# The attention of two layers issued in an order written by hand, with pieces of the output projection between its steps

## The chip, the cores and the metric

The kernel runs on one core of a Trainium2 chip. Its engines work side by side: TensorE (PE) does matmuls and transposes, VectorE (DVE), ScalarE (ACT) and GpSimd (POOL) do arithmetic on tiles in SBUF and PSUM, and SyncE (SP) issues the transfers between DRAM and SBUF. Each engine takes its own instructions strictly in order, and an instruction waits until the semaphores it names have reached their values. The metric is the time of one execution in microseconds (us). Three runs of the kernel before gave 2439.22, 2440.98 and 2441.18 us; the median, 2440.98, is the time before.

## The reference

A trunk of two layers works on 1024 positions of 1024 channels in f32. A layer has two halves: a token mixer and a ConvFFN. Cut to the mixer:

```python
mod = (c_act @ w_ada[l] + b_ada[l])[:, None, :]
sh1, sc1, g1, sh2, sc2, g2 = jnp.split(mod, 6, axis=-1)
h = x * (1.0 + sc1) + sh1
z = h @ w_in[l] + b_in[l]
z_a, z_q, z_k, z_v, z_c = jnp.split(z, splits, axis=-1)
y_a = conformer_conv(z_a, ...)            # 256 wide
y_b = diff_attention(z_q, z_k, z_v, ...)  # 512 wide: 4 heads of 128
y_c = chunked_spatial_gating(z_c, ...)    # 256 wide
y = jnp.concatenate([y_a, y_b, y_c], axis=-1) @ w_out[l] + b_out[l]
x = layer_norm(DEEPNORM_ALPHA * x + (1.0 + g1) * y, ...)
```

The differential attention takes, for each of its four heads and each block of 128 queries, two causal softmax maps p0 and p1 over the keys up to that block, forms a = p0 - lambda * p1, multiplies by v, and normalises each row of the head's output by its root mean square. The ConvFFN then uses sh2, sc2 and g2 in the same way. The six parts of `mod` are called modulation 0 to 5.

## The kernel before

Matmuls run on 512 columns, and each f32 product is made of three (`mm3`: high by high, low by high, high by low), for which operands are split into a high and a low part: ScalarE casts the high part (L125), and POOL or VectorE subtracts it to get the low part (L126). So every weight tile of the output projection, `wout`, is loaded by a transfer on SP's queue (L681), multiplied on POOL by the gate row (L682), cast on ScalarE to `woh`, and subtracted on POOL to `wol`.

`stage1` makes the projections, the convolution and the gating, then q and k of heads 0 to 2, rotated and written to DRAM (`qk_head`: z, `rot`, VectorE at L520 to L524). Its background work (`self.bg`, advanced by `pump`) is a mix of the convolution's taps (L410) and, in layer 0, of modulations 2 and 4: for each modulation eight tiles `wada` of 512 KB are loaded and accumulated on VectorE into `macc` (the first at L258, the others at L260), and `modp` on PE sums the result.

`attention` is a generator that writes out one unit at a time. A unit is one head and one block of 128 queries, i from 0 to 7, with i + 1 key tiles. Its steps: scores `sc` on PE (L733, and a mask at L735), maxima `mx` on VectorE (L754 or L756), exponentials `p` with row sums on ScalarE (L759), the difference on VectorE (L762 to L767), transposes `at` on PE (L774) with copies on ScalarE (L775), the product with v, `pv`, on PE (L778), and two activations on ScalarE (L780, L781). The blocks come in the order 7, 6, 3, 5, 2, 4, 1, 0; in head 3 7, 6, 5, 4, 0, 1, 2, 3. After a head `head_end` normalises, and turns its output by PE transposes `obt` (L801). The heads' q and k come back from DRAM as `stq` and `stk`, v as `vp`. Modulation 3 of layer 0 is loaded and accumulated beside heads 1 to 3. In the midst of heads 2 and 3 the turned heads 0 and 1 (`ybr`, L811) and the four last `wout` are loaded and split.

`stage3` then writes out the rest: the first four `wout` tiles are split, residual rows `r` are loaded and in layer 0 added to a row `ab` on POOL (L871), and `out_fill` adds part of the output projection to them in 512-column halves: 16 pieces of 12 matmuls (`of`; operands `yah`, `yal`, `ych`, `ycl`), then 16 pieces of 6 (`ybh`, `ybL`), each followed by one VectorE operation (L862). What remains, `og`, belongs to the next stage (`boundary`). Head 3's k projection, `prf`, 48 matmuls, stands behind head 0's first unit.

This text order is not the order of issue. The framework's scheduler orders the instructions of all engines by priorities and by estimated times; the `fill` argument and `issue_after` guide it. So a matmul of a piece is put wherever the scheduler sees PE free.

## Time and profile before

| | |
|---|---|
| median of 3 runs | 2440.98 us |
| profiled execution | 2437.79 us |
| its span, first to last instruction | 2436.1 us |
| mean granted clock of PE | 0.974 |
| PE, DVE, ACT, POOL busy | 95%, 80%, 43%, 13% |
| attention of layer 0, first score to first `og` | 286.05 to 507.06 us |
| attention of layer 1, first score to first `og` | 1492.04 to 1708.22 us |

A row of the timeline gives start, length, engine, line, operation, output and inputs, and in brackets the idle time before it with what ended that. Matmul records overlap their successors, so the distance of two starts tells how long one occupies PE, and the sum of the records tells more than that. A row of the table by windows gives the stretch, its length, then the busy time of PE, PEld, DVE, ACT and POOL with counts, PE's granted clock (1.00 is full), the share of the DMA engines in use and GB/s. With a filter on a tile or an engine it counts only those instructions.

### The profile page before, as it was taken

The page shows a single profiled execution, that of the slowest core. Times are in us where ns is not written, and L with a number is a line of the kernel's source. Part 1 is how long each engine was busy: PE and PEld are TensorE (multiplying, and loading weights), DVE is VectorE, ACT ScalarE, POOL GpSimd, SP SyncE. Part 2 cuts the span into 40 slices and gives each one's busy share as a digit, 9 for nine tenths or more (in the row PEclk, how much of TensorE's full clock was granted, in tenths as well). Part 3 has the DMA queues.
Part 4 walks back from the last instruction along what each step waited for, and adds up shares of the span by engine and source line. Part 5 has one row for each costly group of instructions (what it writes and reads, how often), then busy time and mean ns, then how long its engine had stood idle before and what let it go on. Part 6 is the DMA issues. An engine that isn't in the chain of part 4 may idle for free.

```text
span 2436.1 us, 28260 instructions
## 1 busy us (share of the span) xinstructions
PE 2308.1 (95%) x10846; PEld 1886.4 (77%) x10846; DVE 1956.1 (80%) x2650; ACT 1049.9 (43%) x1692; POOL 328.9 (13%) x165
## 2 busy tenths in 40 slices
PE   8998999979999999999959999999899999999996
PEld 7787778767888887788848877777688888878885
DVE  7898876778887888877978988657987777797857
ACT  4214754646554555311130257555654555561111
POOL 1143260410000000000020541214100000000003
PEclk9998999999999999999979999999999999999998
DMA  7433462122332333745523244320232222254301
GB/s 294 156 116 120 140 224 104 61 95 90 110 113 88 112 113 121 263 141 179 190 70 117 78 143 160 130 95 27 99 100 87 78 78 87 87 176 169 122 26 69
DMA packets 87672, 294.06 MB, mean 121 GB/s; under 512 B 9265, under 2 KB 18801, under 8 KB 86001
## 3 DMA queue, kind: packets, MB, share of 16 engines
q1 hardware_dynamic: 87536, 292.26, 35.4%
q8 instruction: 85, 1.39, 0.2%
q14 instruction: 51, 0.41, 0.1%
HBM read 228.23 MB, written 64.00 MB: 120 GB/s over the span
## 4 chain that ended last, share of the span: by engine, by line
PE 67%; DVE 17%; issue 6%; ACT 4%; DMA 3%; POOL 2%; SPq 0%; POOLq 0%; DVEq 0%; ACTq 0%
PE upb L1083 6%; PE upb L1084 6%; PE upb L1085 6%; PE og L130 5%; PE og L131 5%; PE og L132 5%; PE sc L733 3%; PE upd L1084 3%; PE upd L1085 3%; PE upd L1083 3%; DVE convacc L410 2%; PE pv L778 2%; PE of L130 2%; PE of L132 2%; PE of L131 2%
## 5 line engine op out<-in xcount | busy, mean ns | idle before, releaser
L1083 PE MATMUL upb<-comb,uw 128*128 128x512 f32 x704 | 274.9, 391 | 9.9 <-DVE upc L1107 5.0
L130 PE MATMUL og<-dn,dn 128*128 128x512 f32 x704 | 275.3, 391 | 2.6 <-ACT r L885 2.1
L131 PE MATMUL og<-dn,dn 128*128 128x512 f32 x704 | 274.5, 390 | 0.0
L132 PE MATMUL og<-dn,dn 128*128 128x512 f32 x704 | 274.3, 390 | 0.0
L1084 PE MATMUL upb<-comb,uw 128*128 128x512 f32 x704 | 274.0, 389 | 0.0
L1085 PE MATMUL upb<-comb,uw 128*128 128x512 f32 x704 | 273.9, 389 | 0.0
L1107 DVE TENSOR_TENSOR uw<-wu,uw 128x512 fp32r<-128x512 f32 x210 | 144.1, 686 | 125.3 <-ACT uw L1110 125.3
L1120 DVE SCALAR_TENSOR_TENSOR cv<-upc,pc,cv 128x1023 f32<-128x1023 f32 (+1 forms) x176 | 225.4, 1280 | 2.9
L138 POOL TENSOR_TENSOR lnrs<-lnrs,mhalf 128x1 f32<-128x1 f32 x32 | 24.8, 779 | 1421.4 <-DVE lnrs L137 1414.9
L887 DVE TENSOR_TENSOR r<-og,r 128x1024 f32<-128x1024 f32 x128 | 155.7, 1218 | 59.0 <-PE og L132 58.4
L410 DVE SCALAR_TENSOR_TENSOR convacc<-convy,pc,convacc 128x1023 f32<-128x1023 f32 (+14 forms) x120 | 176.2, 1469 | 2.3
L125 ACT CAST dn<-actr 128x1024 fp32r<-128x1024 f32 x44 | 46.1, 1049 | 298.1 <-issue 224.4
L1083 PEld LDWEIGHTS upb<-comb,uw 128*128 128x128 f32 x704 | 132.1, 188 | 41.0 <-DVE upc L1107 6.7
L1110 ACT CAST uw<-wu 128x512 fp32r<-128x512 f32 x210 | 121.7, 616 | 83.6 <-DVE wu L1107 77.1
L130 PEld LDWEIGHTS og<-dn,dn 128*128 128x128 f32 x704 | 132.2, 188 | 31.5 <-ACT r L885 3.4
L1085 PEld LDWEIGHTS upb<-comb,uw 128*128 128x128 f32 x704 | 132.2, 188 | 27.5
L132 PEld LDWEIGHTS og<-dn,dn 128*128 128x128 f32 x704 | 132.2, 188 | 27.4
L1084 PEld LDWEIGHTS upb<-comb,uw 128*128 128x128 f32 x704 | 132.2, 188 | 27.2
L131 PEld LDWEIGHTS og<-dn,dn 128*128 128x128 f32 x704 | 132.2, 188 | 26.8
L1083 PE MATMUL upd<-comb,uw 128*128 128x512 f32 x352 | 137.3, 390 | 0.0
L1085 PE MATMUL upd<-comb,uw 128*128 128x512 f32 x352 | 136.9, 389 | 0.0
L1084 PE MATMUL upd<-comb,uw 128*128 128x512 f32 x352 | 136.9, 389 | 0.0
(312 smaller groups left out, 5474.4 us busy)
## 6 DMA issues: line engine op xcount, KB each, us to landing
wada<-in_w_ada SPq DMA_DIRECT2D x96, 512.0 KB, 4.6
wu<-in_w_up_t SPq DMA_DIRECT2D x84, 512.0 KB, 3.6
d_act<-cv SPq DMA_DIRECT2D x44, 512.0 KB, 2.6
actr<-d_act SPq DMA_DIRECT2D x44, 512.0 KB, 4.6
wdn<-in_w_down SPq DMA_DIRECT2D x44, 512.0 KB, 4.2
win<-in_w_fm SPq DMA_DIRECT2D x24, 512.0 KB, 4.0
wtm<-in_w_tm SPq DMA_DIRECT2D x16, 512.0 KB, 3.7
wout<-in_w_out SPq DMA_DIRECT2D x16, 512.0 KB, 6.2
```

The costliest lines, as they stand in the source:

```text
L130: mm(ps, lh, rh, start=first, stop=False)
L131: mm(ps, lh, rl, start=False, stop=False)
L132: mm(ps, ll, rh, start=False, stop=last)
L410: nc.vector.scalar_tensor_tensor(out=acc[:, d:], in0=y[:, :S - d], scalar=w(30 - d), in1=acc[:, d:], op0=ALU.mult, op1=ALU.add)
L733: nc.tensor.matmul(ps[m][:, c0:c1], q[ms, isl], k[ms, c0:c1], start=n == 0, stop=n == 2 and c1 != w)
L887: nc.vector.tensor_tensor(out=r[t], in0=ps, in1=r[t], op=ALU.add)
L1083: mm(ps, w[:, 0, ks], hi[k], start=k == 0 and not more, stop=False, skip_group_check=True)
L1084: mm(ps, w[:, 0, ks], lo[k], start=False, stop=False, skip_group_check=True)
L1085: mm(ps, w[:, 1, ks], hi[k], start=False, stop=k == 3, skip_group_check=True)
L1107: v.tensor_tensor(out=o, in0=x, in1=y, op=op)
L1110: act.copy(self.up_w[n][:, 0], src)
L1120: v.scalar_tensor_tensor(out=u[:, d:], in0=c[:, :S - d], scalar=self.ffw[:, 2 - d, m:m + 1], in1=u[:, d:], op0=ALU.mult, op1=ALU.add)
```

## The change

The whole attention is written out inside a block, `manual_schedule`, that makes PE, ScalarE and VectorE take their instructions in the order of the program text. The old unit is taken apart into functions: `att_score`, `att_max`, `att_exp`, `att_diff`, `att_turn`, `att_out`. A loop over 32 units (g = 0 to 31) issues, for unit g and the one before it, prev: scores(g), difference(prev), maxima(g), transposes(prev), exponentials(g), a piece, pv(prev), and for some units a second piece. The pieces are, in units 0 to 5, chunks of head 3's k projection (`key_chunks`); in 6 and 7 nothing; in 8 to 19 the 16 pieces of 12 matmuls, two each in 8, 10, 12 and 14; in 20 to 23 nothing; in 24 to 31 the 16 pieces of 6, two each. The late weight tiles and the turned heads 0 and 1 are loaded and split in units 20 to 23. `stage3` is gone.

In layer 0 modulation 4 leaves the background of `stage1` and goes behind modulation 3 in the attention: eight loads of 512 KB and eight VectorE accumulations, one step a unit from unit 8 on. SP and POOL are still ordered by the scheduler.

```diff
@@ -634,7 +634,7 @@
         self.drain_bg()
         if l == 0:
             self.mod_cfg = ("Rb", "Rb")
-            self.bg.append(self.mix(self.mods(0, (2, 4)), self.conv_taps(l, self.y[0], self.acc[0], 0)))
+            self.bg.append(self.mix(self.mods(0, (2,)), self.conv_taps(l, self.y[0], self.acc[0], 0)))
         else:
             self.bg.append(self.conv_taps(l, self.y[0], self.acc[0], 0))
         self.stage_v(l, H, O)
@@ -661,13 +661,14 @@
         self.lhs_a(O)
         vp = self.load_vp(l, 0)
         self.lhsB, self.lhs0, self.wB = [], [], []
-        self.at = O + "c"
-        att = self.attention(l, self.X, O, stk, vp, grow)
         self.qk_head(l, 3, H, O, 0, (0,))
-        next(att)
-        self.qk_head(l, 3, H, O, 0, (1,), True)
-        self.at = self.X + "c"
-        return att, grow
+        wk = self.load_win(l, ZT["k"] + 3, O + "b")
+        self.wA = []
+        with self.tc.manual_schedule(engines={nc.tensor.engine, nc.scalar.engine, nc.vector.engine}):
+            r = self.attention(l, H, self.X, O, stk, vp, grow, wk)
+        self.psum(3, 2)
+        self.up_first(l, O + "c")
+        return r, self.lhsB, self.wB[2:]
 
...
+    def att_max(self, u):
...
+    def att_score(self, u, stk):
+        u["w"] = (u["i"] + 1) * P
+        u["small"] = u["i"] < 4
+        if u["small"]:
+            ps2 = u["ps2"] = self.mm("sc")
+            u["ps"] = [ps2[:, 0:512], ps2[:, 512:1024]]
+        else:
+            u["ps"] = [self.mm("sc"), self.mm("sc")]
+        self.score(u["ps"], stk, u["i"])
+
+    def att_exp(self, u):
...
+    def att_diff(self, l, u):
...
+    def att_turn(self, u, at):
...
+    def att_out(self, u):
...
+    def head_norm(self, ot, ss, halves):
...
+    def head_scale(self, ot, ss, halves):
...
+    def head_turn(self, l, h, O, ot, halves):
...
+    def key_chunks(self, l, h, H, w):
+        nc = self.nc
+        m = ZT["k"] + h
+        hi, lo = w
+        bias = self.col(l, "bin", m)
+        z, rot = self.page("raw", "z"), self.page("Rb", "rot")
+        for half in range(2):
+            sl = slice(half * 512, (half + 1) * 512)
+            pb = self.bank("prf", "fill")
+            for k in range(KT):
+                ks = slice(k * P, (k + 1) * P)
+                self.mm3(pb, hi[:, ks], lo[:, ks], H[0][k][:, sl], H[1][k][:, sl], k == 0, k == KT - 1)
+                if k == 3:
+                    yield
+            nc.scalar.activation(out=z[:, sl], in_=pb, func=AF.Identity, bias=bias)
+            self.rotate(rot[:, sl], pb, bias, 1.0)
+            yield
+        nc.vector.tensor_tensor(out=z, in0=z, in1=self.trig[0], op=ALU.mult)
+        nc.vector.tensor_tensor(out=rot, in0=rot, in1=self.trig[1], op=ALU.mult)
+        yield
+        nc.vector.tensor_tensor(out=z, in0=z, in1=rot, op=ALU.add)
+        nc.scalar.copy(rot.bitcast(F32R), z)
+        nc.vector.tensor_tensor(out=z, in0=z, in1=rot, op=ALU.subtract)
+        for x, t in enumerate((rot, z)):
+            nc.sync.dma_start(self.d_k[l][h, :, x, :], t)
+        yield
+
+    def fill_chunks(self, lhs, w, r, tiles, scale=1.0):
+        for t in tiles:
+            yield from self.out_fill_steps(lhs, w, r, t, scale)
+
+    def attention(self, l, H, X, O, stk, vp, grow, wk):
+        nc = self.nc
+        r = {}
+        order = (4, 5, 0, 1, 2, 3, 6, 7)
+        keys = self.key_chunks(l, 3, H, wk)
+        fillA = self.fill_chunks(self.lhsA, self.wA, r, order, 1.0 if l else ALPHA)
+        fill0 = self.fill_chunks(self.lhs0, self.wB, r, order)
+        raws = ab = pend = None
+        late = iter(())
+
+        def finish(u):
+            self.att_diff(l, u)
+
+        units = [(h, n, i) for h in range(4)
+                 for n, i in enumerate((7, 6, 3, 5, 2, 4, 1, 0) if h < 3 else (7, 6, 5, 4, 0, 1, 2, 3))]
+        prev = None
+        heads = {}
+        for g, (h, n, i) in enumerate(units):
+            if n == 0:
+                heads[h] = (self.page("rows" if h else "raw", "ot", shape=(P, NT, P)), self.sm("oss", [P, NT]))
+                if h:
+                    stk, vp = nxt, nvp
+            ot, ss = heads[h]
+            u = {"i": i, "vp": vp, "ot": ot, "ss": ss}
+            self.att_score(u, stk)
+            if prev:
+                self.att_diff(l, prev)
+            self.att_max(u)
+            if prev:
+                self.att_turn(prev, (O if g < 6 else X) + "c")
+            self.att_exp(u)
+            fills = keys if g < 6 else fillA if g < 20 else fill0
+            if not 6 <= g < 8 and not 20 <= g < 24:
+                next(fills, None)
+            if prev:
+                self.att_out(prev)
+            if g in (8, 10, 12, 14) or g >= 24:
+                next(fills, None)
+            if h and n == 1:
+                self.head_norm(*heads[h - 1], (0, 1))
+            if h and n == 2:
+                self.head_scale(*heads[h - 1], (0, 1))
+                self.head_turn(l, h - 1, O, heads[h - 1][0], (0, 1))
+            if h == 3 and n == 5:
+                self.head_norm(ot, ss, (1,))
+            if h == 3 and n == 6:
+                self.head_scale(ot, ss, (1,))
+                self.head_turn(l, h, O, ot, (1,))
+            if g == 4:
+                if l == 0:
+                    ab = self.page("rows", "ab")
+                    nc.sync.dma_start(ab, self.gab(0, 0, 1))
+                raws = self.page(X + "a", "wout", shape=(P, 4, 1024))
+                for k in range(len(self.woA), 4):
+                    self.woA.append(self.scaled_wout(l, KA[k], grow, raws[:, k - 2]))
+            if 4 <= g < 8:
+                self.wA.append(self.split_wout(O, self.woA[g - 4]))
+            if h == 0:
+                t = order[n]
+                r[t] = self.load_res(t, ab) if n >= 5 else None
+                if n == 5:
+                    for t in order[:5]:
+                        r[t] = self.load_res(t, ab)
+            if h == 1 and n == 0 and l == 0:
+                self.mod_cfg = (None, None)
+                mt = self.page(X + "a", "wada", shape=(P, 4, 1024))
+                self.mod_tile = [mt[:, j] for j in range(4)]
+                late = self.mods(0, (3, 4))
+            if n == (1 if h else 6) and h + 1 < 4:
+                nxt = self.load_stacks(l, h + 1, X)
+                nvp = self.load_vp(l, h + 1)
+            if g in (20, 21):
+                self.lhs0.append(self.load_yb(l, g - 20, O))
+            if 20 <= g < 24:
+                self.wB.append(self.load_wout(l, g - 18, O, grow, self.page(O + "a", "wout")))
+            next(late, None)
+            prev = u
+        self.att_diff(l, prev)
+        self.att_turn(prev, X + "c")
+        next(fill0, None)
+        self.att_out(prev)
+        self.head_norm(ot, ss, (0,))
+        for _ in fillA:
+            pass
+        for _ in fill0:
+            pass
+        self.head_scale(ot, ss, (0,))
+        self.head_turn(l, 3, O, ot, (0,))
         if l == 0:
             for _ in late:
                 pass
             self.affine_cols(0, 1)
+        return r
+
+    def out_fill_steps(self, lhs, w, r, t, scale):
+        nc = self.nc
+        ts_ = slice(t * P, (t + 1) * P)
+        lhs = lhs[:4]
+        for n in range(2):
+            ns = slice(n * 512, (n + 1) * 512)
+            pb = self.bank("of", "fill")
+            for k in range(len(lhs)):
+                self.mm3(pb, lhs[k][0][:, ts_], lhs[k][1][:, ts_], w[k][0][:, ns], w[k][1][:, ns], k == 0,
+                         k == len(lhs) - 1)
+            nc.vector.scalar_tensor_tensor(out=r[t][:, ns], in0=r[t][:, ns], scalar=scale, in1=pb, op0=ALU.mult,
+                                           op1=ALU.add)
+            yield
 
...
-    def stage3(self, l, H, O, att):
...
@@ -1365,8 +1459,7 @@
             if l:
                 self.psum(2, 3, 1)
             self.X = X
-            att = self.stage1(l, H, Y, pre)
-            r, lhsB, wB = self.stage3(l, X, Y, att)
+            r, lhsB, wB = self.stage1(l, H, Y, pre)
             H2 = self.boundary(l, 0, lhsB, wB, r, X)
             nxt = self.ffn(l, H2, Y, X)
             if nxt:
```

Three places show how the instructions move. The first is POOL in layer 0, between the conversion of the group norm's output and the end of head 0. `yal` and `wol` are low parts, `wout` a weight tile multiplied by the gate row, `r` a residual row. Before:

```order
L126 TENSOR_TENSOR yal_2107<-ya_2011,yah_2106 128x1024
L126 TENSOR_TENSOR wol_2321<-wout_1666,woh_2320 128x1024
L126 TENSOR_TENSOR wol_2325<-wout_1798,woh_2324 128x1024
L126 TENSOR_TENSOR yal_2111<-ya_2024,yah_2110 128x1024
L682 TENSOR_TENSOR wout_2315<-wout_2315,grow_1664 128x1024 x2
L126 TENSOR_TENSOR wol_2329<-wout_2315,woh_2328 128x1024
```

After:

```order
L126 TENSOR_TENSOR yal_2072<-ya_1976,yah_2071 128x1024
L683 TENSOR_TENSOR wout_2428<-wout_2428,grow_1629 128x1024 x2
L989 TENSOR_TENSOR r_2487<-r_2487,ab_2426 128x1024
L989 TENSOR_TENSOR r_2490<-r_2490,ab_2426 128x1024
L989 TENSOR_TENSOR r_2496<-r_2496,ab_2426 128x1024
L126 TENSOR_TENSOR wol_2434<-wout_1631,woh_2433 128x1024
L126 TENSOR_TENSOR wol_2484<-wout_1763,woh_2483 128x1024
L989 TENSOR_TENSOR r_2493<-r_2493,ab_2426 128x1024
L126 TENSOR_TENSOR yal_2076<-ya_1989,yah_2075 128x1024
L126 TENSOR_TENSOR wol_2544<-wout_2428,woh_2543 128x1024
L989 TENSOR_TENSOR r_2499<-r_2499,ab_2426 128x1024
L989 TENSOR_TENSOR r_2502<-r_2502,ab_2426 128x1024
```

The first two `wol`, which stood ahead of the late `wout`, now stand behind both of its scalings and three `r`; the fourth, `wol_2587`, comes right behind the last row shown.

The second place is PE in unit 8, the first unit of head 1, with the first piece. Before, the first piece came in ones and twos between other work; one such stretch:

```order
L735 MATMUL sc_2525<-maskb,identb 128x128
L131 MATMUL of_3781<-wol_2329,ych_1632 128x512 [waits Pool_49]
L132 MATMUL of_3781<-woh_2328,ycl_1633 128x512
L130 MATMUL of_3781<-woh_2332,ych_1648 128x512 [waits Activation_49]
L778 MATMUL pv_2419<-vp_2114,at_2412 128x128 [waits Activation_49]
```

After, the piece is one block between the transposes and pv of unit 7:

```order
L792 MATMUL at_2620<-ident,p_2577 128x128 [waits DVE_49]
L130 MATMUL of_2628<-woh_2433,yah_2071 128x512
L131 MATMUL of_2628<-wol_2434,yah_2071 128x512 [waits Pool_49]
L132 MATMUL of_2628<-woh_2433,yal_2072 128x512
L130 MATMUL of_2628<-woh_2483,yah_2075 128x512
L131 MATMUL of_2628<-wol_2484,yah_2075 128x512 [waits Pool_49]
L132 MATMUL of_2628<-woh_2483,yal_2076 128x512 [waits Pool_49]
L130 MATMUL of_2628<-woh_2543,ych_1597 128x512
L131 MATMUL of_2628<-wol_2544,ych_1597 128x512 [waits Pool_49]
L132 MATMUL of_2628<-woh_2543,ycl_1598 128x512
L130 MATMUL of_2628<-woh_2586,ych_1613 128x512 [waits Activation_49]
L131 MATMUL of_2628<-wol_2587,ych_1613 128x512 [waits Pool_49]
```

All four `wol` are waited for inside the block, and nothing else of PE can pass.

The third place is ScalarE in units 20 to 23, where `ybr` and the late `wout` are cast. Before:

```order
L759 ACTIVATE p_3405,sums_3401<-sc_3403,mx_3402 128x1024 [waits DVE_49]
L125 CAST woh_3238<-wout_3235 128x1024 [waits Pool_49]
L759 ACTIVATE p_3406,sums_3401<-sc_3404,mx_3402 128x1024 [waits DVE_49]
L775 COPY at_3354<-at_3355 128x256 [waits PE_49]
L780 ACTIVATE ot_3006<-pv_3313,rc_3298 128x128 [waits PE_49]
L781 ACTIVATE pv_3313,oss_3007<-ot_3006 128x128 [waits Activation_49]
L759 ACTIVATE p_3465,sums_3461<-sc_3463,mx_3462 128x896 [waits DVE_49]
L125 CAST woh_3330<-wout_3327 128x1024 [waits Pool_49]
```

After, at the end of unit 22 and in unit 23:

```order
L803 ACTIVATE pv_3542,oss_3129<-ot_3128 128x128 [waits Activation_49]
L125 CAST woh_3553<-wout_3550 128x1024 [waits Pool_49]
L793 COPY at_3575<-at_3576 128x256 [waits PE_49]
L769 ACTIVATE p_3580,sums_3581<-sc_3559,mx_3573 128x128 [waits DVE_49]
L769 ACTIVATE p_3580,sums_3581<-sc_3559,mx_3573 128x128
L802 ACTIVATE ot_3128<-pv_3584,rc_3568 128x128 [waits PE_49]
L803 ACTIVATE pv_3584,oss_3129<-ot_3128 128x128 [waits Activation_49]
L125 CAST woh_3592<-wout_3589 128x1024 [waits Pool_49]
L793 COPY at_3624<-at_3625 128x128 [waits PE_49]
L769 ACTIVATE p_3628,sums_3630<-sc_3600,mx_3621 128x1024 [waits DVE_49]
```

Each unit's cast now stands ahead of the copy of that unit's transposes and of the next exponentials; before, the casts of the four `wout` stood two units later, among the exponentials of head 3.

More of the change, by code (lines that the diff above doesn't have):

```diff
@@ L747, in attn_unit @@
-            pr = [p2[:, 0:512], p2[:, 512:1024]]
-        else:
-            ps = [self.mm("sc"), self.mm("sc")]
-            pr = [self.page("tmp", "p") for _ in range(2)]
-        self.score(ps, stk, i)
+            pr = u["p"] = [p2[:, 0:512], p2[:, 512:1024]]
+        else:
+            pr = u["p"] = [self.page("tmp", "p") for _ in range(2)]
+        sums = u["sums"] = self.sm("sums", [P, 2], bufs=4)
         for m in range(2):
-            if not small:
-                nc.vector.tensor_reduce(out=mx[:, m:m + 1], in_=ps[m][:, :w], axis=AX.X, op=ALU.max, negate=True)
@@ L755, in attn_unit @@
[L755 to L759 removed]
+            nc.scalar.activation(out=pr[m][:, :w], in_=u["ps"][m][:, :w], func=AF.Exp, bias=u["mx"][:, m:m + 1],
                                  accum_out=sums[:, m:m + 1])
[L761 removed]
+    def att_diff(self, l, u):
+        nc = self.nc
+        w, sums = u["w"], u["sums"]
+        rc = u["rc"] = self.sm("rc", [P, 2], bufs=4)
@@ L814, in load_yb @@
         return hi, lo
-    def attention(self, l, H, O, stk, vp, grow):
-        pend = None
-        for h in range(4):
-            ot = self.page("rows", "ot", shape=(P, NT, P))
-            ss = self.sm("oss", [P, NT])
-            for n, i in enumerate((7, 6, 3, 5, 2, 4, 1, 0) if h < 3 else (7, 6, 5, 4, 0, 1, 2, 3)):
-                self.attn_unit(l, self.at, stk, vp, i, ot, ss)
-                if n == 1 and pend:
-                    self.head_end(*pend)
-                if h >= 1 and l == 0:
-                    if n == 0 and h == 1:
-                        self.mod_cfg = (None, None)
-                        mt = self.page(H + "a", "wada", shape=(P, 4, 1024))
-                        self.mod_tile = [mt[:, i] for i in range(4)]
-                        late = self.mods(0, (3,))
-                    with self.tc.issue_after(self.unit_end.ins):
-                        next(late, None)
-                if n == (1 if h else 4) and h + 1 < 4:
-                    nxt = self.load_stacks(l, h + 1, H)
-                    nvp = self.load_vp(l, h + 1)
-                k = {(2, 3): 0, (2, 5): 1, (2, 7): 2, (3, 0): 3}.get((h, n))
-                if k is not None:
-                    if k < 2:
-                        self.lhs0.append(self.load_yb(l, k, O))
-                    self.wB.append(self.load_wout(l, 2 + k, O, grow, self.page(O + "a", "wout")))
-                if h == 3 and n == 4:
-                    self.head_end(l, h, O, ot, ss, (1,))
-                yield
-            pend = (l, h, O, ot, ss)
-            stk, vp = nxt, nvp
-        self.head_end(*pend, (0,))
@@ new lines, in key_chunks @@
+    def key_chunks(self, l, h, H, w):
+        nc = self.nc
+        m = ZT["k"] + h
[22 more added lines that the diff above has]
+        yield
```

82 lines of the change are left out of this document (25 added, 57 removed).

## The prediction

> **What bounds the kernel now.** I read the page's head first, then its chain of waits, then the two attention stretches (first score to first matmul of the last projection group `og`) in the table by windows.
>
> ```profile
> span 2436.1 us, 28260 instructions
> PE 2308.1 (95%) x10846; PEld 1886.4 (77%) x10846; DVE 1956.1 (80%) x2650; ACT 1049.9 (43%) x1692; POOL 328.9 (13%) x165
> PE 67%; DVE 17%; issue 6%; ACT 4%; DMA 3%; POOL 2%; SPq 0%; POOLq 0%; DVEq 0%; ACTq 0%
> 286.05:507.06 221.01, 206.43 (x1170) 162.85 (x1169) 156.62 (x221) 124.98 (x317) 75.32 (x31) 0.95 0.33 115
> 1492.04:1708.22 216.18, 202.87 (x1153) 158.80 (x1153) 141.85 (x210) 124.94 (x318) 54.20 (x23) 0.97 0.27 98
> ```
>
> PE carries the end. In a window row the first number is the length, then PE, PEld, DVE, ACT, POOL busy, then the granted clock. PE looks 93% busy in both stretches, but a busy record is not full speed, so I count work instead. Starts at full rate:
>
> ```profile
> 288.46 0.39 PE L130 MATMUL prf<-h,wh 128*128 128x512 f32 x1
> 293.01 0.39 PE L132 MATMUL prf<-h,wl 128*128 128x512 f32 x1
> 339.64 1.65 PE L733 MATMUL sc<-stk,stq 64*128 64x512 f32 x6
> 341.29 0.89 PE L778 MATMUL pv<-vp,at 128*128 128x128 f32 x6
> 360.86 1.05 PE L778 MATMUL pv<-vp,at 128*128 128x128 f32 x8
> 361.75 0.60 PE L774 MATMUL at<-ident,p 128*128 128x128 f32 x4
> 362.18 1.06 PE L778 MATMUL pv<-vp,at 128*128 128x128 f32 x8
> ```
>
> Twenty 512-column matmuls lie between 288.46 and 293.01: 0.2275 each. One map's scores of eight key tiles take 1.65 (339.64 to 341.29), so 0.41 a tile for two maps; eight pv matmuls 0.89 and four transposes 0.43, so 0.11 a tile each. A head has 36 key tiles: 36 x 0.63 = 22.7. The stretch also holds the `of` matmuls of the fill pieces and 48 `prf` ones of a key projection. The `of` ones by head (PE busy, with the count in brackets):
>
> ```profile
> 286.05:337.90 51.85, 4.53 (x10) 0.84 0.55 197
> 337.90:390.00 52.10, 24.93 (x98) 1.00 0.44 148
> 390.00:440.07 50.07, 21.61 (x85) 1.00 0.28 99
> 440.07:507.06 66.99, 26.71 (x96) 0.97 0.11 37
> ```
>
> Work of layer 0: 4 x 22.7 + (289 + 48) x 0.2275 = 167.5 of 221.0. The rest, 53.5, is slack: waiting and slow clock. By heads: 51.85 - 22.7 - 58 x 0.2275 = 16.0; then 7.1, 8.0 and 22.5. Layer 1: 216.2 - 167.5 = 48.7. The change can win at most about 100 us here; it loses if its own slack is larger. The count of PE's work is unchanged, so the sum is a sum of slack.
>
> **Part 1, units 0 to 7.** Now VectorE does head 3's query rotation (L520 to L524) ahead of the first maximum, and ScalarE the four `rot` ahead of the first exponential.
>
> ```profile
> 289.89 1.12 ACT L518 ACTIVATE z<-prj,qb 128x1024 f32<-128x1024 f32 x1
> 291.04 4.47 ACT L380 ACTIVATE rot<-prj,qb 32x1024 f32<-32x1024 f32 x4
> 296.80 3.35 DVE L522 TENSOR_TENSOR z<-z,rot 128x1024 f32<-128x1024 f32 x1
> 297.89 1.11 ACT L759 ACTIVATE p<-sc,mx 128x1024 f32<-128x1024 f32 x1
> 303.55 1.23 DVE L524 TENSOR_TENSOR z<-z,rot 128x1024 f32<-128x1024 f32 x1 [0.44 <-ACT rot L523]
> 286.00:338.00 52.00, 46.19 (x226) 35.03 (x225) 39.82 (x43) 40.96 (x76) 27.85 (x11) 0.84 0.55 197
> 308.72 10.71 DMA wout<-in_w_out
> ```
>
> L522 ends at 300.15, 14.1 after the first score; then a cast (about 1), L524 1.23 and the maximum (about 1.2): first exponential at about 17, against 11.8 (297.89) before. The second map's was at 303.54 before, so the unit itself is not later. But ScalarE was busy 40.96 in head 0; less the 5.6 spent on z and rot, 35.4 follow in fixed order, to 52, and the casts of units 6 and 7 stand behind the two late `wout`: asked for at 308.72 before, 22.7 after the first score, and on their way 10.7. The key chunks now end in unit 3, so I set their landing at 44 and the scores of unit 8 at 61. Slack 61 - 22.7 - 10.9 = 27; I take 26. Ends: 16 as before, and 32. Layer 1 has the same rows: 25.
>
> **Part 2, the gate at unit 8.** PE now stops at the first fill piece until the last `wol` of the weights is written; before, its matmuls lay one or two at a time between scores.
>
> ```profile
> 317.26 2.46 POOL L126 TENSOR_TENSOR yal<-ya,yah 128x1024 fp32r<-128x1024 f32 x1 [18.19 <-ACT yah L125]
> 319.69 6.51 POOL L682 TENSOR_TENSOR wout<-wout,grow 128x1024 f32<-128x1024 f32 x2
> 326.15 2.81 POOL L126 TENSOR_TENSOR wol<-wout,woh 128x1024 fp32r<-128x1024 f32 x1
> 328.92 8.62 POOL L871 TENSOR_TENSOR r<-r,ab 128x1024 f32<-128x1024 f32 x3
> 337.50 2.38 POOL L126 TENSOR_TENSOR wol<-wout,woh 128x1024 fp32r<-128x1024 f32 x1
> 339.85 13.41 POOL L871 TENSOR_TENSOR r<-r,ab 128x1024 f32<-128x1024 f32 x5
> ```
>
> All four `wol` now stand behind the two scalings and between the residual sums: 2 scalings 6.5, six `r` 16.5 (8.62 + 13.41 over 8 each), four `wol` 10.4 (2.81 and 2.38), one `yal` 2.5 make 35.9. From 44 that is 80; PE arrives at 61 + 3.3 of scores = 64. Stall 16; I take 13, since the ends lie below it more than above: 5 when `wout` lands as early as before (319.4, so 33.4 + 35.9 = 69), 18 when two us later. Queued behind that matmul are pv, the next scores and so both other engines. Layer 1 adds no `ab` (POOL is 21 us lighter there): 2.
>
> **Part 3, units 8 to 19.** All 16 pieces of 12 matmuls lie here. Heads 1 and 2 had 7.1 + 8.0 slack in 16 units; 12 units of it are 11, and PE has a piece between most steps. But nothing can overtake: turned heads wait in order. I take 10 in each layer, ends 5 and 14.
>
> **Part 4, units 20 to 23.** No piece is left here, and ScalarE has six casts of loaded `ybr` and `wout` in its fixed order, ahead of the copies and exponentials of these units. Before, the same chain ran so:
>
> ```profile
> 434.40 0.32 SPq L811 DMA_DIRECT2D ybr<-d_yb  x1
> 436.67 10.29 SPq L681 DMA_DIRECT2D wout<-in_w_out  x3
> 459.63 1.03 ACT L125 CAST woh<-wout 128x1024 fp32r<-128x1024 f32 x1
> ```
>
> From issue to the end of the last cast 26.3. It cannot begin sooner, since its pages are those that the last piece of unit 19 reads. Four units of 3, 5, 2 and 1 tiles are 6.9 of PE work that cover it. So 26.3 - 6.9 = 19.4, and in layer 0 SP has modulation loads and a key stack ahead: 20 there, 16 in layer 1 where nothing else is in the queue. Ends 10 (casts that wait only for the first `wout`) and 26.
>
> **Part 5, head 3 and the end.** Head 3 had 22.5, which held that chain's wait and the end. Now 96 `of` matmuls go two pieces to a unit: I take 8 and 7, ends 3 and 12. At the end no piece is left under the last unit's chain:
>
> ```profile
> 495.81 0.50 PE L130 MATMUL of<-woh,ybh 128*128 128x512 f32 x1 [1.84 <-DVE r L862]
> 496.57 1.01 POOL L138 TENSOR_TENSOR oss<-oss,mhalf 128x4 f32<-128x4 f32 x1 [13.54 <-DVE oss L137]
> ```
>
> Before, pieces ran on through it, some after a wait for VectorE, 1.84 at most. Now difference, transposes, copy, pv, two activations, norm (1.01 on POOL) and scaling follow each other, some eleven steps of 0.3 to 1.0 us: 7, ends 4 and 10.
>
> **Part 6, the moved modulation.** Eight accumulations leave the stage ahead of attention, where VectorE does not pause (the group is that of 170 to 220 us):
>
> ```profile
> L260 DVE SCALAR_TENSOR_TENSOR macc<-wada,cact,macc 128x1024 f32<-128x1024 f32 x7 | 10.0, 1422 | 0.0
> 220.00:230.00 10.00, 8.99 (x31) 6.80 (x31) 7.12 (x17) 8.52 (x8) 0.00 (x0) 0.57 0.19 71
> ```
>
> The seven take 10.0, and the eighth is the product that starts them. PE falls behind VectorE there and runs at clock 0.57 afterwards, so I take 8 saved, ends 0 (PE's other work covers them) and 11. In attention they cost nothing by themselves: VectorE is 71% busy there (156.62 of 221.01). Without that cover they would cost their 10.0.
>
> **The sum.** Slack of layer 0: 26 + 13 + 10 + 20 + 8 + 7 = 84 against 53.5, so +30. Layer 1: 25 + 2 + 10 + 16 + 7 + 7 = 67 against 48.7, so +18. Saved -8. Together +40: the profiled execution took 2437.8 (its span and 1.7 around it), so 2478. The median shown is 3.2 above that execution; I make no correction for it.
>
> **Rivals.** *The order pays.* If `wout` lands early and each cast finds its data, the parts sit near their lower ends: layer 0 18 + 5 + 6 + 12 + 3 + 5 = 49, layer 1 18 + 0 + 6 + 11 + 3 + 5 = 43, saved 8: 4.5 + 5.7 + 8 = 18 gained, 2420. It decides where the chain of Part 4 takes under 19 us in place of 26.3. For it: heads 1 and 2 already lose only 7 to 8 each with pieces between steps. Against: the 26.3.
>
> *Only one gate bites.* Early `wout` and a short Part 4 (14 and 11), the rest as forecast: 40 - 8 - 6 - 5 = 21 more, 2459.
>
> *The clock falls too.* After waits of 2.17 and 1.60 us PE ran slow:
>
> ```profile
> 295.56 1.77 PE L733 MATMUL sc<-stk,stk 64*128 64x512 f32 x6 [2.17 <-ACT rot L380]
> 303.09 0.63 PE L131 MATMUL prf<-h,wh 128*128 128x512 f32 x1
> 303.52 0.63 PE L132 MATMUL prf<-h,wl 128*128 128x512 f32 x1
> 307.53 0.40 PE L130 MATMUL prf<-h,wh 128*128 128x512 f32 x1
> ```
>
> Starts stand 0.43 apart until 307.3, eight us from 299.15, which costs 3.7. Three more such waits a layer (gate, Part 4, end) add 22: 2500. The Trainium skill, "TensorE: Matmul & The Clock Gate", Part 1, says that PE falls to half speed after an idle window of about 3.4 us and is back after some 3.4 us of work. The trace shows the fall after shorter idles and a slow stretch twice as long; by the page's figure an estimate of 1.7 for each wait would make it 2488.
>
> *The change does nothing.* The scheduler's order was bound by the same chains, so the same waits only change their names: 2438.
>
> **Chances.** Forecast 0.38, clock 0.19, one gate 0.16, order pays 0.21, nothing 0.06. The measurement tells 0.2% (4.9 us) from no change. So faster 0.21, same 0.06, slower 0.73. The range reaches down to 2425, leaving out half of the faster case, and up to 2512, the clock case with the upper end of the gate and of Part 4; the likeliest case's own range is 2462 to 2494.
>
> **What would show it.** Right: the first `of` waits over 8 us on POOL `wol` in layer 0 and under 5 in layer 1; between units 20 and 24 PE idles over 12 us in each layer, released by ScalarE copies or VectorE behind casts; no `of` follows the last `pv`; POOL's `r` sums lie between `wol`. Wrong: the stretches of 221 and 216 shrink, the wait at the first `of` is under 3 us, or PE's slack in units 20 to 23 is under 10. The stage ahead of attention should be 8 shorter; if it is not, Part 6 is wrong alone.

## The result, and the profile after

The changed kernel takes 2546.5 us (median of four runs, 2544.7 to 2547.5) against 2440.1 for the kernel before (its median with one more run, taken beside the new ones): a ratio of 1.0437, 95% interval 1.0419 to 1.0455. It is 106 us slower. The forecast had the side right, slower by 40, but 2546 lies outside its range, which ended at 2512.

The head of the page of the changed kernel, its shares by engine, and its chain of waits:

```profile
span 2543.0 us, 28268 instructions
PE 2300.6 (90%) x10846; PEld 1882.4 (74%) x10846; DVE 1947.9 (77%) x2650; ACT 1057.2 (42%) x1692; POOL 327.1 (13%) x165
PE 64%; DVE 18%; issue 6%; ACT 4%; DMA 3%; POOL 3%; SPq 0%; POOLq 0%; DVEq 0%; ACTq 0%
```

The same number of matmuls and nearly the same busy time (2308.1 before); PE's share falls because the span grew. The table by windows, cut at the attention of both layers (first score to first `og`), and then layer 0 by the parts of the forecast: units 0 to 7; unit 8 to the scores of unit 9; from there to the end of the last piece of 12; to the scores of unit 24; to the transposes of unit 31; to `og`.

```profile
276.71:565.44 288.73, 207.92 (x1186) 165.01 (x1185) 162.45 (x230) 128.45 (x317) 75.58 (x31) 0.84 0.30 102
1552.95:1811.77 258.82, 195.50 (x1153) 154.41 (x1153) 138.82 (x211) 128.32 (x317) 50.62 (x23) 0.89 0.22 80
...
276.71:339.78 63.07, 42.76 (x244) 33.26 (x243) 39.95 (x45) 43.57 (x88) 25.54 (x10) 0.77 0.43 157
339.78:357.16 17.38, 11.13 (x44) 8.02 (x43) 4.91 (x5) 5.08 (x12) 15.70 (x7) 0.74 0.54 194
357.16:451.08 93.92, 80.27 (x483) 65.60 (x482) 52.43 (x81) 35.09 (x95) 4.55 (x2) 0.95 0.33 106
451.08:485.38 34.30, 15.76 (x96) 12.26 (x94) 22.01 (x26) 16.17 (x43) 23.06 (x9) 0.65 0.48 167
485.38:555.92 70.54, 54.52 (x311) 42.92 (x312) 37.92 (x65) 25.50 (x72) 5.72 (x4) 0.90 0.03 8
555.92:565.44 9.52, 3.48 (x17) 2.95 (x17) 5.23 (x10) 3.04 (x7) 1.01 (x1) 0.56 0.00 0
```

The first two rows answer to the two stretches of 221.0 and 216.2 before: 67.7 and 42.6 longer. The first score comes at 276.7 in place of 286.1, so the stage ahead of attention is 9.3 shorter. Together that is +101 of the 106.9 by which the span grew; of the rest some 4 lie behind the attentions, where `og` starts at a lower clock.

The waits of PE in layer 0's attention, by who ended them (total, times, longest):

```profile
PE at L792 <- DVE p L781: 30.5, 20, 6.1
PE pv L800 <- ACT at L793: 19.2, 9, 7.3
PE obt L829 <- DVE ot L814: 11.2, 5, 5.4
PE sc L734 <- ACT rot L380: 8.3, 1, 8.3
PE of L131 <- POOL wol L126: 5.8, 1, 5.8
```

Largest is the wait of the transposes `at` for VectorE's difference (L781). The forecast had no term of its own for it. Of the 30.5 us, 7.2 lie in units 0 to 7, behind VectorE's rotation of head 3's keys, 11.2 in units 8 to 19, 1.6 in units 20 to 23 and 10.5 from there on. Before, no wait of `at` for the difference is among the totals of that layer; PE was idle for 14.6 us of its attention (the stretch less PE's busy time), and is now for 80.8.

### The profile page after: what moved, and what is told of

Same layout as the page of the kernel before. It is cut to its first block, busy times and chain, and to the rows that moved or that the text cites. A ratio compares the mean times of both kernels' runs of the same rounds, so it can differ in the third digit from the quotient of the medians.

```text
span 2543.0 us, 28268 instructions
## 1 busy us (share of the span) xinstructions
PE 2300.6 (90%) x10846; PEld 1882.4 (74%) x10846; DVE 1947.9 (77%) x2650; ACT 1057.2 (42%) x1692; POOL 327.1 (13%) x165
## 4 chain that ended last, share of the span: by engine, by line
PE 64%; DVE 18%; issue 6%; ACT 4%; DMA 3%; POOL 3%; SPq 0%; POOLq 0%; DVEq 0%; ACTq 0%
PE upb L1177 6%; PE upb L1178 6%; PE upb L1179 6%; PE og L130 5%; PE og L131 5%; PE og L132 5%; PE upd L1178 3%; PE upd L1177 3%; PE upd L1179 3%; PE of L130 2%; PE of L131 2%; PE pv L800 2%; PE of L132 2%; PE upa L1177 1%; PE upa L1178 1%
## 5 line engine op out<-in xcount | busy, mean ns | idle before, releaser
L1177 PE MATMUL upb<-comb,uw 128*128 128x512 f32 x704 | 275.5, 391 | 11.2 <-ACT upe L1270 4.8
L1204 ACT CAST uw<-wu 128x512 fp32r<-128x512 f32 x210 | 121.6, 615 | 84.0 <-DVE wu L1201 77.5
L979 DVE SCALAR_TENSOR_TENSOR r<-r,of 128x512 f32<-128x512 f32 x64 | 43.9, 687 | 133.2 <-PE of L132 126.0
L1177 PE MATMUL upd<-comb,uw 128*128 128x512 f32 x352 | 137.2, 390 | 0.0
L1179 PE MATMUL upd<-comb,uw 128*128 128x512 f32 x352 | 137.0, 389 | 0.0
```

The lines of the kernel that those rows point to most:

```text
L1177: mm(ps, w[:, 0, ks], hi[k], start=k == 0 and not more, stop=False, skip_group_check=True)
L1179: mm(ps, w[:, 1, ks], hi[k], start=False, stop=k == 3, skip_group_check=True)
L1204: act.copy(self.up_w[n][:, 0], src)
```

## The experiments

**The order given back.** Three runs keep the changed text and take engines out of the hand-laid order: all three (e1), VectorE alone (e2), VectorE and ScalarE (e6).

```diff
-        with self.tc.manual_schedule(engines={nc.tensor.engine, nc.scalar.engine, nc.vector.engine}):
+        if True:                                                                    # e1
+        with self.tc.manual_schedule(engines={nc.tensor.engine, nc.scalar.engine}): # e2
+        with self.tc.manual_schedule(engines={nc.tensor.engine}):                   # e6
```

> The changed program text, but without the hand-laid order: the scheduler orders PE, ScalarE and VectorE again (the loads, pages and pieces stay where the change wrote them). Theory A, the fixed order costs (each unit's chain of maximum, exponential, difference and the casts stand in line, and PE cannot pass): back to 2430 to 2455. Theory B, the places where the text puts loads, pages and pieces cost (late weight tiles behind pages that the last piece of 12 reads): stays at 2500 or above, with a wait of 15 us or more between the pieces of 12 and those of 6. Theory C, the slow clock after waits is most of it: between, 2460 to 2490.

> The change with VectorE given back to the scheduler; PE and ScalarE keep the hand-laid order. If VectorE's fixed order is the cause (difference of the unit before ahead of the maxima, sums of pieces between them): 25 us or more faster than the change, 2495 to 2520. If PE's and ScalarE's order is the cause: within 10 us of the change's 2546.

> Only PE keeps the hand-laid order; ScalarE and VectorE are the scheduler's. With VectorE alone freed it took 2490, with all three freed 2460. If ScalarE's order with its casts between the units costs what is left: 2460 to 2472. If PE's own order does (pieces that cannot move, none in units 20 to 23): 2480 to 2492.

Measured: e1 2459.8 (ratio to before 1.0075, 1.0059 to 1.0092), e2 2490.0 (1.0207, 1.0191 to 1.0222), e6 2476.6 (1.0141, 1.0124 to 1.0158). The table by windows for the attentions of e1, cut as above:

```profile
276.88:522.15 245.27, 221.26 (x1186) 174.34 (x1185) 171.80 (x233) 126.53 (x318) 77.29 (x31) 0.90 0.34 121
1504.80:1733.22 228.42, 210.76 (x1153) 166.06 (x1153) 137.92 (x210) 126.63 (x318) 50.24 (x23) 0.93 0.26 93
```

So 87 of the 106 us are the fixed order, and 20 stay in the changed text. Freeing the engines one after the other gives 56 for VectorE, then 13 for ScalarE, then 17 for PE; in another order of freeing the split could differ.

e1 is some 5 us above theory A's window, at the lower edge of C's and far below B's. The gap between its pieces of 12 and of 6 is 11 and 9 us, where B wanted 15 or more. Against C speaks that PE's idle time in the two attentions falls from 80.8 and 63.3 us in the change to 24.0 and 17.7 in e1, while the price of the slow clock falls little. An estimate of that price, PE's busy time in windows of 1 us times what the granted clock lacks of 1.00, gives 29 and 19 us in the change, 24 and 16 in e1, and 9 and 6 before. By that estimate the fixed order cost waiting in the main, and some 7 us of clock; in the 20 us that stay the slow clock may well have a part. The attention of layer 0 is as long in e1 (245.3) as in the kernel before with only the modulation moved (243.3, e8 below); why that of layer 1 is 12 us longer than before, no run shows. Of the other two runs, e2 and e6 each lie a few us outside the windows written for them, e2 on the far side of VectorE's, e6 between the two. The order of VectorE, which the forecast hardly looked at, is the largest single part.

**What in VectorE's order.** In the changed text a unit's difference is written at the start of the next unit. On VectorE it so stands behind the sums `r` of both pieces of its own unit, and each sum waits for matmuls that PE has yet to run. The timelines of ScalarE, VectorE and PE around one unit of head 3 in the changed kernel (start, length, operation, and in brackets the idle time before it):

```profile
535.36 0.47 ACT L769 ACTIVATE p<-sc,mx 128x256 f32<-128x256 f32 x1
536.13 0.69 DVE L979 SCALAR_TENSOR_TENSOR r<-r,of 128x512 f32<-128x512 f32 x1 [1.27 <-PE of L132]
538.57 0.69 DVE L979 SCALAR_TENSOR_TENSOR r<-r,of 128x512 f32<-128x512 f32 x1 [1.75 <-PE of L132]
539.95 0.48 DVE L781 SCALAR_TENSOR_TENSOR p<-p,rho 128x256 f32<-128x256 f32 x1
540.49 0.44 PE L792 MATMUL at<-ident,p 128*128 128x128 f32 x2 [1.03 <-DVE p L781]
```

The exponentials end before 536. VectorE is idle for 1.75 us, waiting for the second piece, while the difference is ready to go; it runs at 539.95, and PE, whose scores are done by then, waits 1.03 for it. The next run moves that one step and leaves all three engines in fixed order:

```diff
-            if prev:
-                self.att_diff(l, prev)
             self.att_max(u)
 ...
                 self.att_out(prev)
+            self.att_diff(l, u)
             if g in (8, 10, 12, 14) or g >= 24:
                 next(fills, None)
```

> The change with one step moved, all three engines still in hand-laid order: a unit's difference is written before the second piece of its own unit, so VectorE no longer has it behind the sums of both pieces, and no longer ahead of the next unit's maxima only. Theory D (VectorE's difference stands behind the sum of a piece that PE has not run yet, which is what giving VectorE back to the scheduler cured): 30 to 50 us faster than the change, 2495 to 2515, most of it in units 24 to 31, which shrink by 12 to 16 us a layer. If it was something else in VectorE's order (rotation at the start, sums of squares): less than 10.

Measured 2496.5 (1.0233, 1.0217 to 1.0248): 50 us faster than the change, near the 56 of giving VectorE up. VectorE's timeline there, for the unit of the same size:

```profile
509.11 0.69 DVE L977 SCALAR_TENSOR_TENSOR r<-r,of 128x512 f32<-128x512 f32 x1 [0.99 <-PE of L132]
509.71 0.16 DVE L776 RECIPROCAL rc<-sums 128x2 f32<-128x2 f32 x1
510.21 0.48 DVE L781 SCALAR_TENSOR_TENSOR p<-p,rho 128x256 f32<-128x256 f32 x1
511.56 0.69 DVE L977 SCALAR_TENSOR_TENSOR r<-r,of 128x512 f32<-128x512 f32 x1 [0.86 <-PE of L132]
```

The difference now lies between the two sums, in what was idle time. From unit 24's first piece to `og` layer 0 shrinks from 76.9 to 60.6 and layer 1 from 72.5 to 59.2; the pieces of 12 take 97 and 85 in place of 108 and 88. PE's waits for the difference fall from 30.5 and 22.7 us to 9.0 and 9.3. The difference consists of VectorE operations alone, so nothing but VectorE's order was changed: theory D stands.

**Other ways at the same wait.** e3 leaves VectorE's order and writes the first piece ahead of the transposes; e4 writes two chunks of the key projection ahead of the first scores.

```diff
+            fills = keys if g < 6 else fillA if g < 20 else fill0      # e3
+            if g >= 8 and not 20 <= g < 24:
+                next(fills, None)
             if prev:
                 self.att_turn(prev, (O if g < 6 else X) + "c")
             self.att_exp(u)
-            fills = keys if g < 6 else fillA if g < 20 else fill0
-            if not 6 <= g < 8 and not 20 <= g < 24:
+            if g < 6:
                 next(fills, None)
 ...
+        next(keys)                                                     # e4
+        next(keys)
         for g, (h, n, i) in enumerate(units):
```

> In units 8 to 19 and 24 to 31 the first piece is written ahead of the transposes of the unit before instead of behind them, so that it covers the chain maximum, exponential, difference on which those transposes wait. If that chain sets the pace of these units: the waits of the transposes on the difference (30.5 us in layer 0, 22.7 in layer 1) fall below 15 and 10, and the time falls by 15 to 30 us. If the clock or ScalarE's casts set it: less than 8 us.

> The first two chunks of head 3's k projection are written ahead of the first scores, so they stand in the wait of 8.25 us that the second map's scores have for ScalarE's rotation. If PE's order at the start costs: 8 to 14 us faster in all (5.5 us of matmuls in each layer, and a faster clock behind them). If units 0 to 7 go at ScalarE's pace (43.6 us busy of 63): 0 to 4.

e3 took 2526.7 (1.0359, 1.0342 to 1.0375), 20 less than the change: a piece under the wait covers part of it. PE's waits for the difference fell to 11.2 and 10.5 us, but those of pv for the copies behind the transposes rose from 19.2 and 17.7 to 27.2 and 25.9, since the piece that had covered these was gone. e4 took 2529.7 (1.0373, 1.0357 to 1.0389), 17 less, more than either theory's window. From the start of the moved chunks to the first piece only 3 and 5 us a layer were won; the rest lies further on and was not traced to a cause.

**Units 20 to 23.** The timelines of ScalarE and POOL in the changed kernel show the casts where the forecast had them:

```profile
465.09 1.04 ACT L125 CAST woh<-wout 128x1024 fp32r<-128x1024 f32 x1 [5.72 <-POOL wout L683]
466.04 0.47 ACT L793 COPY at<-at 128x384 f32<-128x384 f32 x1
475.72 1.04 ACT L125 CAST woh<-wout 128x1024 fp32r<-128x1024 f32 x1 [5.73 <-POOL wout L683]
476.67 0.74 ACT L793 COPY at<-at 128x512 f32<-128x512 f32 x2
```

Twice a copy stands behind a cast that waits 5.7 for POOL, and PE's pv waits for the copies, 14.6 us in these units of layer 0 and 12.9 in layer 1. Is it the place of the casts, or the chain itself? In e12 (with the difference moved) all six casts come two units later; the loads and scalings stay where the text has them.

```diff
             if g in (20, 21):
 ...
             if 20 <= g < 24:
-                self.wB.append(self.load_wout(l, g - 18, O, grow, self.page(O + "a", "wout")))
+                keep.append(self.scaled_wout(l, g - 18, grow, self.page(O + "a", "wout")))
+            if g in (22, 23):
+                raw, hi, lo = keepy.pop(0)
+                self.split(hi, lo, raw)
+                self.lhs0.append((hi, lo))
+            if 22 <= g < 26:
+                self.wB.append(self.split_wout(O, keep.pop(0)))
```

> The hand-laid order with the difference moved (the run that took 2497), and the casts of the turned heads and of all four late weight tiles two units later, in units 22 to 25; their loads and POOL's scaling stay where they are. If ScalarE's place for the casts is what holds units 20 to 23: the waits of pv on the copies (6.3 and 5.3 us a layer) go, the gap between the last piece of 12 and the first of 6 falls from 36 and 32 us to below 26, and the time is 2475 to 2488. If the chain of the first two tiles (load, POOL, cast, POOL) sets the start of the pieces of 6 by itself: the wait only moves to those pieces, the gap stays above 30, and the time within 6 us of 2497.

Measured 2501.7 (1.0244, 1.0214 to 1.0273), against 2496.5 with the casts in place. The waits of pv on the copies fell from 18.5 to 8.2 in layer 0, and PE reached the pieces of 6 seven to nine us sooner; there it then met the wait for `wol`. From the last piece of 12 to `og`, e5 first and then e12:

```profile
436.38:532.78 96.40, 68.82 (x424) 54.58 (x422) 61.75 (x100) 44.66 (x123) 29.56 (x13) 0.83 0.19 66
1671.30:1762.70 91.40, 66.72 (x408) 52.30 (x406) 54.48 (x93) 44.54 (x123) 27.12 (x13) 0.87 0.12 38
```

```profile
437.74:534.98 97.24, 72.61 (x423) 56.72 (x422) 68.24 (x100) 44.73 (x123) 29.12 (x13) 0.85 0.19 66
1678.95:1770.38 91.43, 67.13 (x408) 52.10 (x406) 56.30 (x93) 44.75 (x123) 27.12 (x13) 0.89 0.10 38
```

96.4 and 97.2, 91.4 and 91.4: the gap shrank to 28 and 23 (the one theory wanted below 26, the other above 30), and the stretch did not shrink, as the other wanted. Neither theory is borne out whole, and POOL's timeline in e12 shows why:

```profile
443.30 2.36 POOL L683 TENSOR_TENSOR wout<-wout,grow 128x1024 f32<-128x1024 f32 x1 [15.78 <-PE pv L800]
445.85 5.71 POOL L683 TENSOR_TENSOR wout<-wout,grow 128x1024 f32<-128x1024 f32 x2 [0.19 <-DMA wout<-in_w_out]
459.42 2.34 POOL L126 TENSOR_TENSOR ybL<-ybr,ybh 128x1024 fp32r<-128x1024 f32 x1 [7.86 <-ACT ybh L125]
```

Three tiles were scaled by 451.56; then POOL stood idle for 7.86 us, until ScalarE came to the cast of the first `ybr`. The first two `wol` came after that, and PE waited 4.2 us for the second of them in layer 0 and 5.6 in layer 1, with a slow clock behind it. So in the change and in e5 the casts stand too early and wait for POOL, and in e12 they stand too late and POOL waits for them. A place between the two was not run; whether the chain of load, POOL, cast, POOL holds this stretch by itself, or the place of the casts does, stays open.

**Repairs together.** e10 adds to e5 the chunks ahead, the casts of only the third and fourth tile later, and two modulation steps a unit.

> Hand-laid order on all three engines with four repairs: the difference written ahead of the second piece (as in the run that took 2497), the first two key chunks ahead of the first scores (worth 17 alone), the casts of the third and fourth late weight tile two units later, units 24 and 25, since only the next stage reads them, and two steps of the moved modulations a unit, so that they end ahead of the late weight tiles. If the parts add: 2497 - 17 - 2 x 6 - 8 = 2460, with the gap between the last piece of 12 and the first of 6 down from 36 and 32 us to below 27. If the late tiles' own chain (loads, POOL, cast of the first two) holds unit 24 anyway: that gap stays above 30, and the time above 2470.

Measured 2494.2 (1.022, 1.0206 to 1.0235). The parts did not add. The gap was 32 us in both layers (36 and 32 in e5), and the time above 2470, as its second theory says; the casts of the first two tiles and of `ybr` stand as early in e10 as in the change, so it does not settle the question of e12 either. The chunks ahead gave 3 and 4 us up to the first piece. And with two modulation steps a unit the pieces of 12 of layer 0 took 106 in place of 97, with a wait of 6.8 us for an accumulation. No order laid by hand on all three engines comes near the kernel before here.

**The clock.** e7 puts spare transposes of the identity into an unused bank in units 6, 7, 20, 21 and 23. Of these the diff shows the last three.

```diff
 ...
+            if g in (20, 21, 23):
+                pb = self.bank("warm", "fill")
+                for x in range(40):
+                    nc.tensor.transpose(pb[:, (x % 4) * P:(x % 4 + 1) * P], self.ident, self.ident)
             self.att_exp(u)
```

> The change with spare transposes of the identity into an unused bank where PE waits longest: 20 and 40 in units 6 and 7 ahead of the transposes, 40 each in units 20, 21 and 23 behind them; nothing of the kernel is left out. If the slow clock behind these waits is a cause of its own: PE's clock from unit 20 to 26 rises from 0.5 to 0.65 to above 0.85, and the time falls by 8 to 18 us. If the slow stretches only lie beside waits on other engines: within 5 us of the change.

Measured 2557.5 (1.0478, 1.0463 to 1.0494), 11 slower than the change and outside both windows. The clock from the last piece of 12 to the first of 6 rose from 0.65 to about 0.8, not to the 0.85 that was wanted. The first row shows that stretch (PE alone), the second one block of spare transposes:

```profile
453.80:495.03 41.23, 30.25 (x231) 0.79 0.41 140
458.09 4.53 PE L912 MATMUL warm<-ident 128*128 128x128 f32 x40
```

The gap grew, 41 and 38 us in place of 38 and 32; behind it layer 0 won 3 us and layer 1 lost 1. But the blocks were badly placed. In layer 0 of the change pv waits 0.46, 7.25, 6.41 and 0.50 us in units 20 to 23: the blocks of units 20 and 23, 4.5 and 5.3 us long, stand where PE hardly waited, and unit 22 has none. So e7 pays for its own transposes and does not tell what a faster clock alone would be worth; that stays open.

**The moved modulation.** e8 is the kernel before with that move alone, e9 the change without it, e11 as e8 with two steps a unit, so that the accumulations end before the late weight tiles.

```diff
-            self.bg.append(self.mix(self.mods(0, (2, 4)), ...))     # e8, e11: of before
+            self.bg.append(self.mix(self.mods(0, (2,)), ...))
-                        late = self.mods(0, (3,))
+                        late = self.mods(0, (3, 4))
                     with self.tc.issue_after(self.unit_end.ins):
                         next(late, None)
+                        next(late, None)                            # e11 alone
 ...
-            self.bg.append(self.mix(self.mods(0, (2,)), ...))       # e9: of the change
+            self.bg.append(self.mix(self.mods(0, (2, 4)), ...))
-                late = self.mods(0, (3, 4))
+                late = self.mods(0, (3,))
```

> The kernel before with the moved modulation alone (modulation 4 behind modulation 3 beside heads 1 to 3; the order left to the scheduler as before). If the stage ahead of attention gains its 9 us and attention takes the eight loads and accumulations at no cost: 2428 to 2434. If attention pays for them: 2436 to 2445.

> The change with modulation 4 back in the stage ahead of attention, all else as in the change. If the move is what the forecast took it for (8 to 9 us saved there, nothing paid in attention): 9 to 12 us slower than the change, 2555 to 2558. If its loads and accumulations collide with the late weight tiles' chain, as in the kernel before with the move alone (attention of layer 0 22 us longer, VectorE's accumulations 3.4 us each beside POOL): 5 to 15 us faster, 2531 to 2541.

> The kernel before with the moved modulation, two steps a unit, so that its 18 steps lie beside heads 1 and 2 and end before the late weight tiles are scaled on POOL. If the 12 us that the move cost alone came from VectorE and POOL meeting in head 3: the stage keeps its 11 us, attention of layer 0 is back to 221 to 226, and the time is 2428 to 2434, faster than both kernels. If the move costs by its transfers on SP's queue or its accumulations wherever they lie: 2440 to 2452.

e8 took 2452.0 (1.0045, 1.0030 to 1.0060), slower than before by 12 and above both of its windows; e9 2538.8 (1.0405, 1.0392 to 1.0418), 8 faster than the change, as its second theory says; e11 2437.6 (0.9992, 0.9982 to 1.0002), no different from before and between its two windows. The stage gains as forecast in all of them, 9 to 11 us. Attention pays. In e8 the attention of layer 0 takes 243.3; its accumulations, a stretch where they meet POOL, and POOL's groups there:

```profile
L260 DVE SCALAR_TENSOR_TENSOR wada<-wada,cact 128x1024 f32<-128x1024 f32 x14 | 26.3, 1880 | 0.0
440.00:460.00 20.00, 16.61 (x51) 11.58 (x51) 16.83 (x13) 8.14 (x24) 15.62 (x7) 0.57 0.29 116
458.06 3.39 DVE L260 SCALAR_TENSOR_TENSOR wada<-wada,cact 128x1024 f32<-128x1024 f32 x1
L682 POOL TENSOR_TENSOR wout<-wout,grow 128x1024 f32<-128x1024 f32 x4 | 10.7, 2708 | 1.7 <-DMA wout<-in_w_out 1.7
```

In e11 the same accumulations and the attention of both layers:

```profile
L260 DVE SCALAR_TENSOR_TENSOR wada<-wada,cact 128x1024 f32<-128x1024 f32 x14 | 17.9, 1278 | 1.2 <-DMA wada<-in_w_ada 1.1
275.63:500.33 224.70, 210.07 (x1186) 165.35 (x1185) 163.94 (x233) 124.53 (x317) 75.13 (x31) 0.95 0.37 132
1486.75:1711.40 224.65, 207.35 (x1153) 161.88 (x1153) 142.72 (x210) 125.48 (x318) 53.28 (x23) 0.95 0.26 94
```

In e8 the four accumulations that run beside an operation of POOL take 3.36 to 3.39 us, the ten others 1.28. Brought forward in e11, they all take 1.28, layer 0 is back to 224.7 and the gain of the stage is kept. But e11 brings the loads forward too, and the four take only some 8 us more than by themselves while the attention of e8 grows by 22: that the meeting with POOL is the whole cost is argued, not shown. Layer 1, which has no modulation in its attention, now takes 224.7 in place of 216.2, and eats most of that gain: the scheduler laid it out differently, and why was not pursued. No version run here beats the kernel before by more than the measurement can tell.

## Why the prediction was wrong

The table sets the slack of the forecast against that of the changed kernel's windows, by the forecast's own count (length less 0.63 a key tile and 0.2275 a 512-column matmul of a piece or of head 3's keys). The gate is what the first piece took beyond its twelve matmuls; the rest of units 8 to 19 is part 3.

| part | layer 0: forecast, measured | layer 1: forecast, measured |
|---|---|---|
| 1, units 0 to 7 | 26, 29.5 | 25, 30.3 |
| 2, gate at unit 8 | 13, 6.7 | 2, 0 |
| 3, units 8 to 19 | 10, 22.5 | 10, 8.4 |
| 4, units 20 to 23 | 20, 27.4 | 16, 21.9 |
| 5, head 3 | 8, 26.0 | 7, 22.5 |
| 5, end | 7, 9.5 | 7, 8.6 |
| sum | 84, 121.6 | 67, 91.7 |

**The step that failed is Part 5's "I take 8 and 7, ends 3 and 12" for head 3.** It missed by 18 and 15.5 us, half of the 66 that the forecast lacks, and lies far above its own upper end. It counted pieces on PE and never laid VectorE's fixed order beside them. e5 shows what was missing: the difference stood behind sums that wait for PE, and moving that one VectorE step gives back 16 and 13 us there. With it moved, head 3 and the end together have 19 and 18 us of slack, against the 15 and 14 that the forecast gave them.

**Part 3** has the same fault with more cover: PE's two long pieces hide most of the chain. In layer 1 it was right. In layer 0 it is 12.5 too small, above its end of 14; e5 wins 11 there and 3 in layer 1, and taking modulation 4 out (e9) shortens that stretch from 108 to 102.

**Part 4** named the right wait and had its price nearly right: 27.4 and 21.9 against 20 and 16, in layer 0 just above the upper end, with PE waiting for copies behind casts that wait for POOL. That the length of the chain alone sets it is not shown: in e12 POOL had its tiles and waited for the casts. In layer 0 the gap falls from 38 to 32, the value of layer 1, when modulation 4 is taken out (e9); the forecast had given 4 us to what stands ahead in SP's queue there.

**Parts 1, 2 and the end** were within their ends. Part 1 came near its number by another route, which is luck: it saw ScalarE's casts held up behind the two late `wout`, but in the trace of layer 0 none of them waits. PE's largest waits there are 8.3 us of the second map's scores for ScalarE's rotation, where `prf` matmuls ran before, and 7.2 for the difference. The gate was half of what was taken: the last `wol` was written 74 us after the first score and not 80, and ten of the piece's twelve matmuls ran ahead of it, so PE waited 5.8 us, between the two signs that the forecast had named (over 8, under 3).

**Part 6** was right on the stage (9.3 against 8) and wrong in "in attention they cost nothing by themselves". The move alone costs 12, and within the change 8. VectorE's busy share of 71% over the whole stretch hid that the late steps lie where POOL works; in the changed kernel three of the accumulations, from 460 us on, took 2.4 to 3.4 us in place of 1.28.

**The rivals.** "The order pays" fell, and so did "only one gate bites" and "the change does nothing": e1 shows 87 us of pure order. "The clock falls too" was right on the fall (0.84 and 0.89 over the attentions, 0.95 and 0.97 before). Its price of some 22 us is neither shown nor refuted: the estimate by windows above gives just over 30 us more in the change than before, which is an upper bound, since PE also runs slowly where something else holds the end; e7 could not price it. The range was too narrow because it took the parts' upper ends one or two at a time. Four were passed together, three of them by one cause, VectorE's order, which sat in two parts and both layers.

## What to carry to other kernels

When an order is fixed by hand, lay it out on every engine, not only on the one that carries the end: for each instruction ask what stands in front of it on its own engine and what that one waits for. A consumer of a later step (here the sum of a piece) must not stand ahead of a producer for the critical engine (here the difference). And before work is moved to a stretch where an engine has time on average, look at who works beside it in the very slices where it will land.

## What the runs showed of the hardware

VectorE's accumulation of two SBUF tiles took 1.28 us by itself and up to 3.39 beside an operation of POOL on SBUF tiles; the mean of the fourteen was 1.88 in e8 and 1.28 in e11. The ends of the two operations go together. Here are the POOL operation beside the accumulation of 458.06 in e8, and the one beside L522 in the kernel before, which took 3.35 us where L521 and L524 took 1.23:

```profile
457.86 2.51 POOL L126 TENSOR_TENSOR wol<-wout,woh 128x1024 fp32r<-128x1024 f32 x1 [1.52 <-ACT woh L125]
296.72 2.35 POOL L126 TENSOR_TENSOR wol<-wout,woh 128x1024 fp32r<-128x1024 f32 x1 [3.50 <-ACT woh L125]
```

POOL ends at 460.37 and 299.07, and VectorE, which began just after POOL, at 461.45 and 300.15: 1.08 us later in both cases. The accumulations of 430.66 and 440.82 in e8 and those of 460.43 and 470.12 in the changed kernel end 1.08 after POOL's operation as well. So in these rows VectorE's operation looks held until POOL's is over, rather than slowed. The difference is held in the same way: that of unit 5 in the changed kernel took 2.46 us for 640 columns and ended 0.68 after POOL's sums `r`. The forecast read the row of L522 as a duration only. The Trainium skill, "GPSIMD Engine Reference", section "1. Specifications", says that GpSimd shares its SBUF interfaces with VectorE, with contention for instructions of two SBUF inputs; the runs agree, with 3.39 us in place of 1.28 at most.
